# Where the operands of the matmuls lie in SBUF modulo 256 bytes, and the order of the high and low products, in a decoder layer

## The chip, the cores and the metric

The kernel runs on one core of a Trainium2 chip. The metric is the device time of one execution in microseconds, lower is better. A core has TensorE (PE: matmuls, and PEld: the loading of weights for them), VectorE (DVE), ScalarE (ACT), GpSimd (POOL) and SyncE (SP, which issues most of the DMAs here). They work from the on-chip memory SBUF, and TensorE writes its sums to PSUM.

## The reference

One step of a decoder with a single layer, for 256 prompt tokens and 8 x 4 sample tokens, all float32. Together they are 288 columns.

```
h = h + 1/2 * SwiGLU(RMSNorm(h))                    # FFN 1: 2048 -> 2 x 5632 -> 2048
z = RMSNorm(h) @ w_in                               # 2048 -> 6144 (+ 8 forget gates)
  conv group : y = B * dwconv3_causal(C * h_c)      # 1024 wide
  FoX group  : softmax(q k^T/sqrt(d) + F_t - F_s) v # 8 heads of 128; sample tokens read a paged cache of 1024
h = h + [norm(conv) | norm(FoX)] @ w_out            # 2048 -> 2048
h = h + 1/2 * SwiGLU(RMSNorm(h))                    # FFN 2
h = h + sigmoid(RMSNorm(h) @ w_g) * (p @ w_p)       # 2048 -> 2048, 256 -> 2048
y = RMSNorm(h)
```

The norms' gains are folded into the operands, and the division by the root mean square is applied behind the matmul, to its result.

## The kernel before, in words

Features lie on the 128 partitions and the 288 tokens along the row, so an operand of 2048 features is 16 blocks of 128 x 288. Each product is made at nearly full float32 precision from three faster ones in the format float32r, whose mantissa is shorter: an operand a is split into a high part (rounded to float32r) and a low part (the rest), and w x is summed as w_hi x_hi + w_hi x_lo + w_lo x_hi. `pair` (line 302) is the loop for that: for 256 output features it walks over chunks of four blocks, and in a chunk over two halves b of 128 output features and the blocks j. For each it issues the three products of lines 328, 329 and 330, each of them one matmul of 288 columns with its own load of 128 x 128 weights. Everything large goes through `pair`: both FFNs (`ffn`, line 380), the input and output projections, the last gate and its projection.

Weights come from DRAM as float32 in tiles of four blocks x 256 columns (`wraw`). `split_weight` (line 282) splits two blocks at a time: ScalarE writes the high part to a tile `whi`, VectorE the low part to a tile `wlo`. Each has five buffers of 2,048 bytes in a row of SBUF, in the pool `wsp`. In `whi` and `wlo` the weights of one matmul are 512 bytes of a row.

The moving operands are split likewise, and stand in these tiles:

- x, the input of a projection: `xh` and `xl`, 16 blocks of 1,152 bytes each (`new_x`, line 208). `make_x` and `x_split` fill them block by block, the high part on ScalarE, the low part on VectorE.
- the inner rows of the FFN: `hh` and `hl`, 8 blocks each, two buffers (`start`, line 387), filled in `up` (lines 408 and 409).
- the outputs of the two token-mixing groups, `zc` and `za`, each block a tile of its own; `zch` and `zcl` of a block are allocated one behind the other, `zah` and `zal` eight tiles of 1,152 bytes apart.
- p, the per-layer input: `ph` and `plo`.

Since 1,152 is four and a half times 256, blocks of one tile begin at 0 and at 128 modulo 256 by turns. In the program before, `whi`, `wlo`, `xh`, `xl`, `hh` and `hl` all begin at 0 modulo 256.

The order of the work is that of the program: a list of steps is run once, and each engine gets its instructions in that order. SyncE loads weights eight tiles ahead, splits run five half tiles ahead. Between the matmuls of `pair`, in the token mixing, stand small matmuls for the attention (lines 750 to 905). `inv_rms` (line 181) forms the mean of squares by a matmul with a matrix of 1/2048: `meanr` in float32r for most norms, and a constant `mean` of the same value, loaded from DRAM, in the last norm (`finish`, line 1149).

Of the kernel before, what the change touches and what calls it, by code (L numbers as in the profile page):

```python
# [16 lines left out]
F32 = mybir.dt.float32  # L17
F32R = mybir.dt.float32r
# [26 lines left out]
HALVES = 5  # L45
MANUAL = False
# [15 lines left out]
def constants():  # L62
# [15 lines left out]
    put("mean", np.full((P, P), 1.0 / D))  # L78
# [15 lines left out]
def build(nc, tc, ctx, A, O):  # L94
# [8 lines left out]
    wsp = pool("wsp", HALVES)  # L103
    drp = pool("drp", space=DRAM)
# [76 lines left out]
    def inv_rms(out, parts, width, load=True, weights=const("mean")):  # L181

        b = ktbank()
        m = b[:, :NT]
        for i, x in enumerate(parts):
            pe.matmul(m, weights, x, start=i == 0, stop=i == len(parts) - 1)
        if load:
            log_tables()
        c = float(D // width)
        s.activation(ra, m, AF.Ln, bias=eps, scale=c)  # L190
        s.activation(out, ra, AF.Exp, scale=-0.5)
        v.scalar_tensor_tensor(ra, out, -0.5 * c, out, ALU.mult, ALU.mult)
        v.scalar_tensor_tensor(ra, m, EPS / c, ra, ALU.add, ALU.mult)
        v.scalar_tensor_tensor(out, ra, 1.5, out, ALU.add, ALU.mult)

    def norm_scale(out, squares, width, chunks, load=False):

        s.activation(sqh, squares, AF.Copy)
        v.tensor_tensor(sql, squares, sqh.bitcast(F32), ALU.subtract)
        defer(lambda: inv_rms(out, [sqh, sql], width, load, meanr), chunks)  # L200
# [6 lines left out]

    def new_x():
        X["hi"] = xp.tile([P, KT, NT], F32R, name="xh", tag="xh")
        X["lo"] = xp.tile([P, KT, NT], F32R, name="xl", tag="xl")  # L210
# [55 lines left out]
    def split_upto(n):  # L266
        while state["split"] < min(n, len(halves)):
# [5 lines left out]
            lo = wsp.tile([P, 2, 256], F32R, name="wlo", tag="wlo")  # L273
# [28 lines left out]
    def pair(src, c0, kts, act, evac, k_of=lambda k: k, late=0, tag="mm", rows_first=False):  # L302
# [4 lines left out]
        for ci, ks in enumerate(chunks):  # L307
            it = weight(src, ks[0], len(ks), c0)

            def fn(ci=ci, ks=ks, it=it, only=None):  # L310
# [7 lines left out]
                for b in range(2):  # L318
                    o = st["ps"][b][:, :NT]
                    for j, k in enumerate(ks):  # L320
# [7 lines left out]
                        pe.matmul(o, hi[:, j % 2, w], xh, start=f, stop=False)  # L328
                        pe.matmul(o, hi[:, j % 2, w], xl, start=False, stop=False)  # L329
# [50 lines left out]
    def ffn(wg, wu, wd, nextgain, work):  # L380
# [3 lines left out]
        for gi, grp in enumerate(groups):  # L384
            firstg = gi == 0 and nextgain == "norm_mix"

            def start():
                H["hi"] = work().tile([P, 8, NT], F32R, name="hh", tag="hh", bufs=2)
                H["lo"] = work().tile([P, 8, NT], F32R, name="hl", tag="hl", bufs=2)
# [754 lines left out]
    def finish():  # L1144
# [3 lines left out]
        for i, c in [(0, 0), (0, 1), (1, 0), (2, 0), (1, 1), (2, 1)]:  # L1148
            pin(pe.matmul(sums[c], const("mean"), parts[i][:, SIDES[c]], start=i == 0, stop=i == 2))
# [88 lines left out]
```

## Time and profile before

| | |
|---|---|
| median of 3 runs | 2324.27 us (2323.92 to 2325.14) |
| the profiled execution | 2325.22 us |
| its span | 2323.4 us |
| TensorE busy | 2309.5 us, 99% |
| weight loads busy | 2254.4 us, 97% |
| VectorE busy | 1345.2 us, 58% |
| ScalarE busy | 1053.3 us, 45% |
| GpSimd busy | 323.4 us, 14% |
| granted TensorE clock, mean | 0.998 of full speed |
| DMA | 443.44 MB, mean 191 GB/s |

An engine's busy time is the time in which at least one of its instructions runs. Matmuls overlap in the pipeline and their ends are modelled, so a matmul's duration is longer than the time from one matmul's start to the next one's, and "99% busy" does not mean that columns stream 99% of the time. How fast matmuls follow each other is read from their start times or from their count in a window. A chain of waits follows the work back from the last instruction, at each step to what released it. `xcount` is the number of instructions in a group.

### The profile page before, as it was taken

The page shows a single profiled execution, that of the slowest core. Times are in us where ns is not written, and L with a number is a line of the kernel's source. Part 1 is how long each engine was busy: PE and PEld are TensorE (multiplying, and loading weights), DVE is VectorE, ACT ScalarE, POOL GpSimd, SP SyncE. Part 2 cuts the span into 40 slices and gives each one's busy share as a digit, 9 for nine tenths or more (in the row PEclk, how much of TensorE's full clock was granted, in tenths as well). Part 3 has the DMA queues.
Part 4 walks back from the last instruction along what each step waited for, and adds up shares of the span by engine and source line. Part 5 has one row for each costly group of instructions (what it writes and reads, how often), then busy time and mean ns, then how long its engine had stood idle before and what let it go on. Part 6 is the DMA issues. An engine that isn't in the chain of part 4 may idle for free.

```text
span 2323.4 us, 44297 instructions
## 1 busy us (share of the span) xinstructions
PE 2309.5 (99%) x17387; PEld 2254.4 (97%) x17387; DVE 1345.2 (58%) x2413; ACT 1053.3 (45%) x1860; POOL 323.4 (14%) x398
## 2 busy tenths in 40 slices
PE   9999999999999999999999999999999999999997
PEld 9999999999999999888888999999999999999997
DVE  7555555555555586456566865555555555555755
ACT  6444444444444453334344554444434444444654
POOL 1020000000000023354445210000000000000110
PEclk9999999999999999999999999999999999999999
DMA  8575555555555556888988555545555555555552
GB/s 268 165 243 164 164 166 163 169 166 164 163 165 165 168 162 232 320 302 291 325 317 294 161 169 159 173 155 172 164 167 164 169 163 164 164 165 168 164 167 92
DMA packets 342865, 443.44 MB, mean 191 GB/s; under 512 B 17424, under 2 KB 306976, under 8 KB 342656
## 3 DMA queue, kind: packets, MB, share of 16 engines
q1 hardware_dynamic: 320944, 366.32, 49.4%
q0 software_dynamic: 20480, 71.67, 8.8%
q8 instruction: 136, 2.23, 0.4%
q10 hardware_dynamic: 1232, 2.62, 0.3%
q14 instruction: 73, 0.60, 0.1%
HBM read 435.48 MB, written 5.07 MB: 190 GB/s over the span
## 4 chain that ended last, share of the span: by engine, by line
PE 99%; DVE 0%; DMA 0%; ACT 0%; SPq 0%; issue 0%; DVEq 0%; ACTq 0%
PE mm L328 31%; PE mm L330 31%; PE mm L329 31%; PE va L817 1%; PE va L750 1%; PE va L328 1%; PE va L330 1%; PE va L329 1%; DMA h<-in_x_dram 0%; DVE h L1164 0%; PE kt L328 0%; PE kt L330 0%; PE kt L329 0%; PE kt L871 0%; PE kt L904 0%; PE kt L895 0%
## 5 line engine op out<-in xcount | busy, mean ns | idle before, releaser
L283 DVE TENSOR_TENSOR wlo<-wraw,whi 128x512 fp32r<-128x512 f32 (+1 forms) x1388 | 976.0, 706 | 795.3 <-ACT whi L283 745.9
L283 ACT ACTIVATE whi<-wraw 128x512 fp32r<-128x512 f32 (+1 forms) x1388 | 868.0, 629 | 929.8 <-PE mm L329 898.0
L328 PE MATMUL mm<-xh,whi 128*128 128x288 f32 x3680 | 1093.5, 297 | 0.0
L329 PE MATMUL mm<-xl,whi 128*128 128x288 f32 x3680 | 1085.6, 295 | 0.0
L330 PE MATMUL mm<-xh,wlo 128*128 128x288 f32 x3680 | 1081.9, 294 | 0.0
L328 PEld LDWEIGHTS mm<-xh,whi 128*128 128x128 f32 x3680 | 689.3, 187 | 15.6 <-issue 13.5
L330 PEld LDWEIGHTS mm<-xh,wlo 128*128 128x128 f32 x3680 | 693.0, 188 | 0.1
L329 PEld LDWEIGHTS mm<-xl,whi 128*128 128x128 f32 x3680 | 690.6, 188 | 0.1
L328 PE MATMUL mm<-hh,whi 128*128 128x288 f32 x1408 | 416.8, 296 | 0.0
L329 PE MATMUL mm<-hl,whi 128*128 128x288 f32 x1408 | 415.4, 295 | 0.0
L330 PE MATMUL mm<-hh,wlo 128*128 128x288 f32 x1408 | 414.0, 294 | 0.0
L401 POOL TENSOR_TENSOR sr<-sg,rs 128x288 f32<-128x288 f32 x88 | 72.0, 819 | 1435.3 <-ACT sg L399 1435.1
L330 PEld LDWEIGHTS mm<-hh,wlo 128*128 128x128 f32 x1408 | 265.2, 188 | 0.0
L329 PEld LDWEIGHTS mm<-hl,whi 128*128 128x128 f32 x1408 | 264.2, 188 | 0.0
L328 PEld LDWEIGHTS mm<-hh,whi 128*128 128x128 f32 x1408 | 263.6, 187 | 0.0
L421 DVE SCALAR_TENSOR_TENSOR h<-mm,h 128x288 f32<-128x288 f32 x192 | 87.3, 455 | 23.3 <-PE mm L330 22.9
L399 ACT ACTIVATE sg<-tg 128x288 f32<-128x288 f32 x88 | 39.0, 444 | 99.3 <-DVE tg L397 99.2
L408 ACT ACTIVATE hh<-hd 128x288 fp32r<-128x288 f32 x88 | 39.2, 445 | 93.3 <-DVE hd L406 93.2
L727 POOL DMA_INDIRECT KT<-in_cache_k_dram,idx x64 | 64.2, 1003 | 117.0 <-DVE idx L162 53.5
L223 POOL TENSOR_TENSOR acc<-acc,sq 128x288 f32<-128x288 f32 x52 | 44.0, 845 | 227.2 <-ACT sq L222 224.7
L250 POOL DMA_INDIRECT page<-in_cache_v_dram,idx x64 | 64.8, 1012 | 69.5 <-PE va L817 46.3
L409 DVE TENSOR_TENSOR hl<-hd,hh 128x288 fp32r<-128x288 f32 x88 | 40.2, 457 | 22.0 <-ACT hh L408 22.0
(248 smaller groups left out, 1324.4 us busy)
## 6 DMA issues: line engine op xcount, KB each, us to landing
wraw<-in_w_ffn_gate_dram SPq DMA_DIRECT2D x172, 512.0 KB, 3.5
wraw<-in_w_ffn_up_dram SPq DMA_DIRECT2D x172, 512.0 KB, 3.5
wraw<-in_w_ffn_down_dram SPq DMA_DIRECT2D x160, 512.0 KB, 3.5
wraw<-in_w_in_dram SPq DMA_DIRECT2D x96, 512.0 KB, 5.2
wraw<-in_w_out_dram SPq DMA_DIRECT2D x32, 512.0 KB, 4.3
wraw<-in_w_ple_gate_dram SPq DMA_DIRECT2D x32, 512.0 KB, 3.5
wraw<-in_w_ffn_down_dram SPq DMA_DIRECT2D x32, 256.0 KB, 2.9
wraw<-in_w_ple_proj_dram SPq DMA_DIRECT2D x8, 256.0 KB, 3.2
```

What stands on the lines that cost most here:

```text
L223: (v if k >= KT - last_on_v else g).tensor_tensor(acc, acc, sq, ALU.add)
L250: g.indirect_dma_start(out=t, out_offset=None, in_=it["src"], in_offset=bass.IndirectOffsetOnAxis(ap=it["rows"], axis=0))
L283: for i in s.activation(hi, x, AF.Copy), v.tensor_tensor(lo, x, hi.bitcast(F32), ALU.subtract):
L328: pe.matmul(o, hi[:, j % 2, w], xh, start=f, stop=False)
L329: pe.matmul(o, hi[:, j % 2, w], xl, start=False, stop=False)
L330: state["product"] = pe.matmul(o, lo[:, j % 2, w], xh, start=False, stop=l)
L399: s.activation(u, t, AF.Silu)
L401: g.tensor_tensor(r, u, rs, ALU.mult)
L408: s.activation(H["hi"][:, k, :], t, AF.Copy)
L409: v.tensor_tensor(H["lo"][:, k, :], t, H["hi"][:, k, :].bitcast(F32), ALU.subtract)
L421: v.scalar_tensor_tensor(h[:, k, :], o, 0.5, h[:, k, :], ALU.mult, ALU.add)
L727: d = g.indirect_dma_start(out=t[:, i].rearrange("p h s -> p (h s)"), out_offset=None, in_=A["cache_k"], in_offset=bass.IndirectOffsetOnAx ...
```

## The change

The high and the low part of x become one tile, `x`, in which the high and the low part of each block lie side by side (2,304 bytes, nine times 256, from one block to the next). The function `both` makes it and returns the two views. The tile has room for a few floats ahead of the first block: 4 (16 bytes) for x and 60 (240 bytes) for the FFN's inner rows, now the tile `hid`. The low weights get a pool of their own, `wlp`, behind a gap of 8 floats (32 bytes). In the program as it is then allocated, modulo 256: every `whi` begins at 0, every `wlo` at 32, the high part of every block of `x` and `hid` at 16 and its low part at 144. The tiles of `zc`, `za` and `p` are made as before; since all that is behind the gap has moved, they begin at 32 or 160, the conv group's high parts at 32 and low parts at 160.

In `pair` the two products with the high weights change places: low x comes first, then high x, then low weights with high x. Only where blocks are asked for one by one (`rows_first`, the first pair of FFN 1) high x stays first. The constant `mean` goes, and the matmuls of the last norm read `meanr`, seen as float32, which holds the same value.

```diff
+LOWS = 8
+BEFORE_X = 4
+BEFORE_H = 60
...
-    put("mean", np.full((P, P), 1.0 / D))
...
     wsp = pool("wsp", HALVES)
+    pool("low").tile([P, LOWS], F32, name="gap")
+    wlp = pool("wlp", HALVES)
...
-    def inv_rms(out, parts, width, load=True, weights=const("mean")):
+    def inv_rms(out, parts, width, load=True):
...
-            pe.matmul(m, weights, x, start=i == 0, stop=i == len(parts) - 1)
+            pe.matmul(m, meanr, x, start=i == 0, stop=i == len(parts) - 1)
...
+    def both(p, name, blocks, before, **k):
+        n = blocks * 2 * NT
+        t = p.tile([P, (before + n + 63) // 64 * 64], F32R, name=name, tag=name, **k)
+        t = t[:, before:before + n].rearrange("p (k s n) -> p s k n", s=2, n=NT)
+        return t[:, 0], t[:, 1]
+
     def new_x():
-        X["hi"] = xp.tile([P, KT, NT], F32R, name="xh", tag="xh")
-        X["lo"] = xp.tile([P, KT, NT], F32R, name="xl", tag="xl")
+        X["hi"], X["lo"] = both(xp, "x", KT, BEFORE_X)
...
-            lo = wsp.tile([P, 2, 256], F32R, name="wlo", tag="wlo")
+            lo = wlp.tile([P, 2, 256], F32R, name="wlo", tag="wlo")
...
-                        pe.matmul(o, hi[:, j % 2, w], xh, start=f, stop=False)
-                        pe.matmul(o, hi[:, j % 2, w], xl, start=False, stop=False)
+                        for x in (xh, xl) if rows_first else (xl, xh):
+                            pe.matmul(o, hi[:, j % 2, w], x, start=f, stop=False)
+                            f = False
                         state["product"] = pe.matmul(o, lo[:, j % 2, w], xh, start=False, stop=l)
...
             def start():
-                H["hi"] = work().tile([P, 8, NT], F32R, name="hh", tag="hh", bufs=2)
-                H["lo"] = work().tile([P, 8, NT], F32R, name="hl", tag="hl", bufs=2)
+                H["hi"], H["lo"] = both(work(), "hid", 8, BEFORE_H, bufs=2)
...
-            pin(pe.matmul(sums[c], const("mean"), parts[i][:, SIDES[c]], start=i == 0, stop=i == 2))
+            pin(pe.matmul(sums[c], meanr.bitcast(F32), parts[i][:, SIDES[c]], start=i == 0, stop=i == 2))
```

TensorE has the same 16,656 products of `pair` before and after, in another order. The first place is the start of the conv half of the output projection, behind a round of the attention's values (`page`). Before:

```order
L330 MATMUL mm<-xh,wlo 128x288
L817 MATMUL va<-page,PT_13098 32x512 x8
L328 MATMUL mm<-zch_11984,whi 128x288
L329 MATMUL mm<-zcl_11985,whi 128x288
L330 MATMUL mm<-zch_11984,wlo 128x288
```

And with the change (a tile's number moves by one, and the high and low part of x bear one name, `x`):

```order
L340 MATMUL mm<-x,wlo 128x288
L826 MATMUL va<-page,PT_13097 32x512 x8
L338 MATMUL mm<-zcl_11984,whi 128x288
L338 MATMUL mm<-zch_11983,whi 128x288
L340 MATMUL mm<-zch_11983,wlo 128x288
```

The low part's product now stands ahead of the high part's with the same weights; the third product keeps its place. The second place is the end of the program on TensorE, the last block of the projection of p and the sums of the last norm. Before:

```order
L328 MATMUL mm<-ph,whi 128x288
L329 MATMUL mm<-plo,whi 128x288
L330 MATMUL mm<-ph,wlo 128x288
L1149 MATMUL kt<-acc,consts 128x144 x2
L1149 MATMUL kt<-sq_27334,consts 128x144
```

And with the change:

```order
L338 MATMUL mm<-plo,whi 128x288
L338 MATMUL mm<-ph,whi 128x288
L340 MATMUL mm<-ph,wlo 128x288
L1158 MATMUL kt<-acc,meanr 128x144 x2
L1158 MATMUL kt<-sq_27325,meanr 128x144
```

The same three products in the new order, and the sums read `meanr` for the constant. VectorE, ScalarE and GpSimd keep all their rows and their order; on SyncE the only row that differs is the load of the constants, 498 columns instead of 626.

More of the change, by code (lines that the diff above doesn't have):

```diff
@@ L199, in norm_scale @@
         v.tensor_tensor(sql, squares, sqh.bitcast(F32), ALU.subtract)
-        defer(lambda: inv_rms(out, [sqh, sql], width, load, meanr), chunks)
+        defer(lambda: inv_rms(out, [sqh, sql], width, load), chunks)
     def split(hi, lo, x, gcol):
```

## The prediction, before the result was known

> **What bounds the kernel now.** I read the summary of engines first, then the chain of work that ended last, then who waited for whom on TensorE, and then the time from one matmul to the next in stretches.
>
> ```profile
> span 2323.4 us, 44297 instructions
> PE 2309.5 (99%) x17387; PEld 2254.4 (97%) x17387; DVE 1345.2 (58%) x2413; ACT 1053.3 (45%) x1860; POOL 323.4 (14%) x398
> PE 99%; DVE 0%; DMA 0%; ACT 0%; SPq 0%; issue 0%; DVEq 0%; ACTq 0%
> ```
>
> The chain is TensorE alone. What TensorE waits for is this, from the view of waits, for the whole span:
>
> ```profile
> PE mm L509 <- DVE fixed L506: 1.2, 1, 1.2
> PE va L328 <- ACT whi L283: 0.8, 1, 0.8
> PE kt L1149 <- ACT sq L1135: 0.7, 1, 0.7
> ```
>
> That is 2.7 us in 2323.4. No wait can give or cost much, so the time is the number of matmuls times the time from one to the next, which I call the pitch. The number comes from the group of weight splits, since each split serves 2 blocks of rows and 2 output halves, 4 times three products:
>
> ```profile
> L283 ACT ACTIVATE whi<-wraw 128x512 fp32r<-128x512 f32 (+1 forms) x1388 | 868.0, 629 | 929.8 <-PE mm L329 898.0
> ```
>
> 1,388 x 4 x 3 = 16,656 matmuls of 288 columns. Their mean duration of 294 to 297 ns is a modelled pipeline time and not the pitch; the pitch is read from a window's length and the matmuls in it (the first number in brackets is TensorE's; two of each count began before the window):
>
> ```profile
> core 0: us, PE busy (x) PEld busy (x) DVE busy (x) ACT busy (x) POOL busy (x), PEclk, DMA share, GB/s
> 100.00:800.00 700.00, 700.00 (x5253) 700.00 (x5252) 377.75 (x623) 305.33 (x512) 39.82 (x46) 1.00 0.55 172
> 1312.00:1356.00 44.00, 44.00 (x332) 44.00 (x332) 38.12 (x70) 26.57 (x56) 9.43 (x12) 1.00 0.52 160
> ```
>
> 700 / 5,251 and 44 / 330 are both 133.3 ns, at a full granted clock (1.00). 16,656 x 133.3 ns = 2,220 us, 96% of the span. The question is what in 133.3 ns is neither columns nor weight load. The last norm of the kernel has matmuls of another kind, two passes over 144 columns, so again 288 column steps, with a weight load of the same 128x128 form before each pass:
>
> ```profile
> 2309.65 0.65 PE L1149 MATMUL kt<-acc,consts 128*128 128x144 f32 x4
> L1149 PE MATMUL kt<-acc,consts x4: 284/286/286, 2309.6 to 2310.0; 128*128 128x144 f32 x4
> ```
>
> Three steps fit in 0.65 us less the last one's 0.286: 121 ns. So neither 288 steps nor the weight load needs 133.3 ns; 12 ns of each of the 16,656 are something else. [...]
>
> **Does the trace before show that addresses matter?** In one stretch it does. In x and the FFN's inner rows the high and the low part stand a multiple of 256 bytes apart, so both have the same place modulo 256 (0 for even blocks, 128 for odd ones). Weights stand at 0. The conv half of the output projection is the exception: zch and zcl are 1,152-byte tiles, one behind the other, so the high part is always at 0 and the low part always at 128. Matmuls in order of time there (start, duration in us):
>
> ```profile
> 1286.69 0.29 PE L329 MATMUL mm<-zcl,whi 128*128 128x288 f32 x1
> ...
> 1288.14 0.29 PE L328 MATMUL mm<-zch,whi 128*128 128x288 f32 x1
> ...
> 1288.53 0.29 PE L328 MATMUL mm<-zch,whi 128*128 128x288 f32 x1
> ...
> 1288.93 0.30 PE L328 MATMUL mm<-zch,whi 128*128 128x288 f32 x1
> ...
> 1292.90 0.29 PE L186 MATMUL kt<-sqh,meanr 128*128 128x288 f32 x1
> ```
>
> From 1286.69 to 1292.90 there are 47 steps: 132.1 ns. Within it a block's three products take 0.39 us (1288.14 to 1288.53) where 3 x 133.3 is 0.40: 130 ns each. The attention half that follows (zah, zal: equal places again) is the 44 us window above, at 133.3 with the same engines beside it. So 133.3 is no fixed cost, and parts 128 apart run a little faster when undisturbed. When disturbed by other matmuls they can run slower. Two steps behind the attention's products (L904, L905) the view shows:
>
> ```profile
> 1251.50 0.29 PE L328 MATMUL mm<-zch,whi 128*128 128x288 f32 x1
> ...
> 1251.91 0.30 PE L328 MATMUL mm<-zch,whi 128*128 128x288 f32 x1
> 1252.04 0.31 PE L329 MATMUL mm<-zcl,whi 128*128 128x288 f32 x1
> 1252.19 0.30 PE L330 MATMUL mm<-zch,wlo 128*128 128x288 f32 x1
> 1252.33 0.29 PE L328 MATMUL mm<-zch,whi 128*128 128x288 f32 x1
> ...
> 1252.72 0.30 PE L328 MATMUL mm<-zch,whi 128*128 128x288 f32 x1
> ```
>
> The block from 1251.91 takes 0.42 us, 140 ns each, and the 9 steps from 1251.50 to 1252.72 take 135.6.
>
> [...]
>
> **The change part by part.**
>
> *Placement of x and the inner rows, of low weights, and low x first.* These act together on 16,656 pitches. The new places modulo 256: high weights 0, low weights 32, high x and inner rows 16, low ones 144 for every block. While a product streams, the next weights load. Before, the distance from loading weights to moving data was 0 or 128 in every such pair. Now it is 144 (low x, high weights coming), then -16 (high x, low weights coming), then +16 (high x, the next high weights). The trace of before shows none of these three distances. Bounds from the nearest rows: at best the excess goes, 121 ns; at worst the slow block is held, 140 ns. Rows in between: 132.1 for a whole stretch with parts 128 apart, 130 for its best blocks. The zc stretch is the nearest row, since it too has the parts 128 apart for every block; but there one distance (0) is left as it was, and here all three are moved, so I let some of the step from 132.1 to 130 be reached: 131.5 ns. 16,656 x (133.3 - 131.5) = 30 us less. Ends: 16,656 x 12.3 = 205 us less, and 16,656 x 6.7 = 112 us more.
>
> *Low x first, as a wait.* A block's first product now waits for the low part, which VectorE makes after ScalarE made the high part. The rows:
>
> ```profile
> L408 ACT ACTIVATE hh<-hd 128x288 fp32r<-128x288 f32 x88 | 39.2, 445 | 93.3 <-DVE hd L406 93.2
> L409 DVE TENSOR_TENSOR hl<-hd,hh 128x288 fp32r<-128x288 f32 x88 | 40.2, 457 | 22.0 <-ACT hh L408 22.0
> ```
>
> Before, the low part was wanted one pitch, 133 ns, after the high one. TensorE has no wait on either in the list above. The cover is the order of blocks: the last inner row is wanted in the second group of four blocks of the down projection, 24 products or 3.2 us after the first, against 0.45 + 0.46 us plus VectorE's step before. Taken at 0; with the cover gone it is 133 ns at each of the 12 groups of the two FFNs and the 3 new x, 2 us. In the kernel's first pair the old order is kept.
>
> *One tile instead of two.* High and low now share a tile, so a new x or a new set of inner rows waits for readers of both. The last reader was already the third product, which reads the high part; VectorE, ScalarE, GpSimd and SyncE keep their rows. 0.
>
> *The constant for the mean.* The table of constants loses 128 of 626 columns, and that DMA stands on SyncE behind the first weights and x. The three sums at the end read another tile with the same value. 0: no wait of TensorE in the list above is on that table, and a smaller transfer only lands earlier.
>
> *A new bound?* A split of weights serves 12 products, 1.6 us now and 1.45 at the best end of 121 ns; ScalarE needs 0.63 of it, and VectorE is 58% busy in all. DMA is at 0.52 to 0.55 in the windows. No.
>
> The sum: the profiled execution took 2325.2 us (span 2323.4 and 1.8 around it); 2325.2 - 30 = 2295, and about 2294 against the median of 2324.3. I predict 2295.
>
> **The rivals.**
>
> *The excess is a fixed cost of such a matmul.* For it: even and odd blocks stand 128 apart before, and both run at 133.3. Against it: 130 and 140 in the zc stretch. Time: 2324, no change; the same follows if the new distances happen to meet as often as the old ones. [...]
>
> *The late cycle takes hold (the other side).* Place: the streams of x and inner rows. If low at 144 and high at 16 settle into what zc shows behind an interruption, the 135.6 ns of those 9 steps hold: 16,656 x 2.3 = 38 us more, 2362. It decides from the point where slow blocks of 140 outnumber gains: 1.8 / (1.8 + 6.7), about one block in five. Against it: interruptions are rare in the FFNs, which have most matmuls, and zc comes back within 12 steps.
>
> [...]
>
> **How the numbers follow.** Forecast (a pitch of 129 to 132.6): 0.60. Fixed cost or no difference: 0.17. Late cycle: 0.14. Clash gone: 0.09. What the measurement can tell from no change is about 0.2%, 5 us. Faster by more: 0.60 + 0.09, and 0.01 from small gains outside, 0.70; same 0.16; slower 0.14. The forecast alone spans 2254 (129 ns) to 2313 (132.6 ns). The range for 8 in 10 leaves out the larger part of the late cycle and most of the vanished clash: 2225 (127.3 ns) to 2333, which takes in no change and a beginning of the late cycle.
>
> **What would show it.** Right: counts of matmuls in the same windows of 700 and 44 us go up by about 1.4%; waits of TensorE stay near 3 us; all other rows keep their durations. The fixed cost: again 5,251 in 700 us. The late cycle: blocks of 0.42 us outside the conv half. The low-first wait: a row of TensorE waiting for L409's successor. The forecast is wrong if the pitch lies outside 129 to 132.6 in the FFN stretches, or if time moves anywhere but in the pitch.

## The result, and the profile after

The changed kernel takes 2297.34 us (median of 4 runs, 2297.28 to 2297.66) against 2324.22 us for the kernel before in the same session: a ratio of 0.9884, 95% interval 0.9867 to 0.9901. 2295 us was forecast, with a range from 2225 to 2333. The profiled execution took 2297.66 us, 27.6 us less than the one of before.

The page of the changed kernel, its span, engines, chain of work and the group of weight splits (compare with the same rows in the prediction):

```profile
span 2295.9 us, 44307 instructions
...
PE 2282.3 (99%) x17387; PEld 2226.8 (97%) x17387; DVE 1346.2 (59%) x2413; ACT 1052.6 (46%) x1860; POOL 323.2 (14%) x398
...
PE 99%; DVE 0%; DMA 0%; ACT 0%; SPq 0%; issue 0%; DVEq 0%
...
L292 ACT ACTIVATE whi<-wraw 128x512 fp32r<-128x512 f32 (+1 forms) x1388 | 867.3, 629 | 907.8 <-PE mm L338 847.0
```

TensorE has the same 17,387 matmuls and the chain is still TensorE alone; the other engines work as long as before, a split still takes 629 ns. TensorE's waits in the changed kernel, for the whole span:

```profile
PE mm L518 <- DVE fixed L515: 1.2, 1, 1.2
PE kt L1158 <- ACT sq L1144: 0.7, 1, 0.7
PE kt L338 <- ACT whi L292: 0.4, 1, 0.4
```

2.3 us where it was 2.7. So the 27 us are not in waits but in the time from one matmul to the next, the pitch. Matmuls in two windows of 700 us of the changed kernel, one in FFN 1 and one in FFN 2 (the number behind "PE busy" is TensorE's count; two of each began before the window):

```profile
core 0: us, PE busy (x) PEld busy (x) DVE busy (x) ACT busy (x) POOL busy (x), PEclk, DMA share, GB/s
100.00:800.00 700.00, 700.00 (x5387) 700.00 (x5386) 392.21 (x649) 314.86 (x535) 43.02 (x50) 1.00 0.56 177
1400.00:2100.00 700.00, 700.00 (x5252) 700.00 (x5251) 380.08 (x629) 306.27 (x512) 29.22 (x36) 1.00 0.54 166
```

And the second window of the kernel before, whose first window is in the prediction (5253):

```profile
1400.00:2100.00 700.00, 700.00 (x5252) 700.00 (x5251) 380.08 (x629) 305.52 (x512) 29.29 (x36) 1.00 0.53 165
```

This is the surprise. Before, both windows run at 700 / 5,251 = 133.3 ns. After, FFN 1 runs at 700 / 5,385 = **130.0 ns** and FFN 2 at 700 / 5,250 = **133.3 ns**, the same as before the change. The code, the places modulo 256 and the order of products are the same in both FFNs. One FFN has gained 3.3 ns a matmul, the other nothing; the mean looks like the forecast. The start times of the norms' matmuls tell the same: that at the end of FFN 1 starts at 859.72 us before and at 838.39 after, 21.3 us earlier; that at the start of FFN 2 at 1357.14 and 1331.79, 25.35 earlier; and that behind FFN 2 at 2202.19 and 2176.86, 25.33 earlier.

Where the pitch changes, the timeline of TensorE in the changed kernel shows (start and duration; each L340 is the last product of a block):

```profile
1331.27 0.29 PE L340 MATMUL va<-x,wlo 128*128 128x288 f32 x1
...
1331.66 0.29 PE L340 MATMUL va<-x,wlo 128*128 128x288 f32 x1
1331.79 0.29 PE L190 MATMUL kt<-sqh,meanr 128*128 128x288 f32 x1
1331.92 0.30 PE L190 MATMUL kt<-sql,meanr 128*128 128x288 f32 x1
...
1332.33 0.30 PE L340 MATMUL va<-x,wlo 128*128 128x288 f32 x1
...
1332.73 0.30 PE L340 MATMUL va<-x,wlo 128*128 128x288 f32 x1
```

Up to the norm at 1331.79 us a block's three products take 0.39 us (1331.27 to 1331.66). Behind the norm's two matmuls they take 0.40 (1332.33 to 1332.73), and they go on so for 835 us, to the end of FFN 2, with no wait between. Each of these two ways of running repeats and holds itself; I call it a cycle. Something small at 1331.79 us chose.

FFN 1 was no different at its start. There, too, the stream ran at 130.0 when the norm's two matmuls came (x3 is three products in a row, whose duration is that of all):

```profile
38.52 0.29 PE L340 MATMUL mm<-x,wlo 128*128 128x288 f32 x1
...
38.91 0.29 PE L340 MATMUL mm<-x,wlo 128*128 128x288 f32 x1
39.03 0.29 PE L190 MATMUL kt<-sqh,meanr 128*128 128x288 f32 x1
39.17 0.30 PE L190 MATMUL kt<-sql,meanr 128*128 128x288 f32 x1
...
45.57 0.30 PE L340 MATMUL mm<-x,wlo 128*128 128x288 f32 x1
...
45.97 0.30 PE L340 MATMUL mm<-x,wlo 128*128 128x288 f32 x1
46.10 0.73 PE L338 MATMUL mm<-x,whi 128*128 128x288 f32 x3
46.67 0.30 PE L340 MATMUL mm<-x,wlo 128*128 128x288 f32 x1
...
49.29 0.29 PE L340 MATMUL mm<-x,wlo 128*128 128x288 f32 x1
...
49.68 0.29 PE L340 MATMUL mm<-x,wlo 128*128 128x288 f32 x1
```

A block takes 0.39 us before this norm and 0.40 behind it, as in FFN 2. But from 46.10 to 46.67 us three steps take 0.57 us where 0.40 is usual (the trace names no wait there), and a few blocks later the stream is back at 0.39 and stays there to the end of FFN 1. So FFN 1 has its 130.0 ns behind an irregular break 7 us after its norm, and FFN 2 met no such break. The norm's two matmuls do not always do the same: at 838.39 us they leave the stream at 130.0, and at 2176.86, behind FFN 2, they put it from 133.3 back to 130.0.

### The profile page after: what moved, and what is told of

Same layout as the page of the kernel before. It is cut to its first block, busy times and chain, and to the rows that moved or that the text cites. A ratio compares the mean times of both kernels' runs of the same rounds, so it can differ in the third digit from the quotient of the medians.

```text
span 2295.9 us, 44307 instructions
## 1 busy us (share of the span) xinstructions
PE 2282.3 (99%) x17387; PEld 2226.8 (97%) x17387; DVE 1346.2 (59%) x2413; ACT 1052.6 (46%) x1860; POOL 323.2 (14%) x398
## 4 chain that ended last, share of the span: by engine, by line
PE 99%; DVE 0%; DMA 0%; ACT 0%; SPq 0%; issue 0%; DVEq 0%
PE mm L338 62%; PE mm L340 31%; PE va L338 1%; PE va L826 1%; PE va L759 1%; PE va L340 1%; PE kt L338 0%; DMA wraw<-in_w_ffn_up_dram 0%; DVE h L1173 0%; PE kt L340 0%; PE kt L880 0%; PE kt L913 0%; PE kt L904 0%; PE kt L879 0%; PE mm L560 0%; PE va L839 0%
## 5 line engine op out<-in xcount | busy, mean ns | idle before, releaser
L338 PE MATMUL mm<-x,whi 128*128 128x288 f32 x7360 | 1459.0, 294 | 0.0
L338 PEld LDWEIGHTS mm<-x,whi 128*128 128x128 f32 x7360 | 1178.4, 188 | 15.8 <-issue 13.5
L340 PE MATMUL mm<-x,wlo 128*128 128x288 f32 x3680 | 1083.0, 294 | 0.0
L340 PEld LDWEIGHTS mm<-x,wlo 128*128 128x128 f32 x3680 | 693.0, 188 | 0.2 <-DVE wlo L292 0.2
L338 PE MATMUL mm<-hid,whi 128*128 128x288 f32 x2816 | 556.5, 294 | 0.0
L338 PEld LDWEIGHTS mm<-hid,whi 128*128 128x128 f32 x2816 | 451.4, 188 | 0.0
L340 PE MATMUL mm<-hid,wlo 128*128 128x288 f32 x1408 | 414.7, 295 | 0.0
L340 PEld LDWEIGHTS mm<-hid,wlo 128*128 128x128 f32 x1408 | 265.2, 188 | 0.0
L418 DVE TENSOR_TENSOR hid<-hd,hid 128x288 fp32r<-128x288 f32 x88 | 40.2, 457 | 22.0 <-ACT hid L417 22.0
L338 PE MATMUL va<-x,whi 128*128 128x288 f32 x256 | 51.5, 294 | 0.0
```

The costliest lines, as they stand in the source:

```text
L338: pe.matmul(o, hi[:, j % 2, w], x, start=f, stop=False)
L340: state["product"] = pe.matmul(o, lo[:, j % 2, w], xh, start=False, stop=l)
L418: v.tensor_tensor(H["lo"][:, k, :], t, H["hi"][:, k, :].bitcast(F32), ALU.subtract)
```

## The experiments

In those kernels that hold matmuls alone (the distances, the map, the sizes and the places) the decoder's work is left out and the outputs are zeros.

### The order alone

```diff
-                        pe.matmul(o, hi[:, j % 2, w], xh, start=f, stop=False)
-                        pe.matmul(o, hi[:, j % 2, w], xl, start=False, stop=False)
+                        for x in (xh, xl) if rows_first else (xl, xh):
+                            pe.matmul(o, hi[:, j % 2, w], x, start=f, stop=False)
+                            f = False
```

(This and nothing else, on the kernel before.)

> The kernel before with low x first and nothing moved. Distance theory: all distances stay 0 or 128, pitch 133.3, 2324 us. Order theory (what gains is that high x follows low x): 2297 us.

2325.62 us against 2325.83, ratio 0.9999 (0.9989 to 1.0009). Low x first costs no wait and gives nothing by itself at the old places.

### The places alone

```diff
-                        for x in (xh, xl) if rows_first else (xl, xh):
+                        for x in (xh, xl):
```

(On the changed kernel: high x first again.)

> The change with high x first. Distance theory: the distances become 16, 112, 16 instead of 144, -16, 16, so another pitch than the change's mix of 130.0 and 133.3; if 16 and 112 act as 0 does, 2324 us, if they are as good, 2297 us. Order theory: no gain without the order, 2324 us.

2304.01 us, ratio 0.9902 (0.9886 to 0.9919). No run took this median: two took 2307.10 and 2307.28 us, two 2300.69 and 2300.92. The trace is of the run of 2307.10. Its window in FFN 2 (FFN 1 has one matmul more):

```profile
1400.00:2100.00 700.00, 700.00 (x5296) 700.00 (x5295) 382.25 (x632) 307.20 (x516) 30.57 (x38) 1.00 0.53 167
```

132.2 ns in both. The places carry most of the gain, 19 to 25 us, and the order matters once the places are moved: with low x first one FFN is faster than this (130.0), the other slower (133.3). So one and the same program had two times here. What the two quicker runs did no trace shows; 6.4 us is about what one FFN, some 6,300 matmuls, would gain at 131.2 ns instead of 132.2, an estimate from the pitch that the next experiment finds for these places.

### Matmuls alone at every distance

```diff
+    def uniform(name, d):
...
+        for k in range(120):
+            mm(o, wt(0, k), mv(d, k))
...
+            for k in range(40):
+                a, b = (lo, hi) if low_first else (hi, lo)
+                mm(o, wt(0, k), mv(a, k))
+                mm(o, wt(0, k), mv(b, k))
+                mm(o, wt(wlo, k), mv(hi, k))
```

(`wt(a, k)` are weights at a modulo 256, `mv(a, k)` 288 columns of moving data at a. First all 120 at one distance, then in threes as in `pair`.)

> The kernel's work is left out here: only runs of matmuls of 288 columns with 128x128 weights in float32r, 120 to a stretch, with the moving operand at a chosen place modulo 256 behind the loading weights. Distance theory (the pitch is set by the place of the moving data against the weights that load meanwhile): the stretch with all at 0 and the one with 128 run at 133.3 ns, the change's places (low 144, high 16, low weights 32, low first) run in one of two cycles, 130.0 or 133.3, and other distances differ; two matmuls of a norm in the middle can switch the cycle, and a norm whose operands stand at the change's places, with three products, cannot. Fixed-cost theory: every stretch at 133.3. Two-pass matmuls of 144 columns: 121 ns in both.

Rows of its timeline, one for 120 matmuls in a row. dd is a distance of 48, dh 112; then threes at the change's places, threes with x at 0 and 128 and low weights at 32, and the two-pass form:

```profile
64.94 15.85 PE L131 MATMUL dd<-op 128*128 128x288 f32 x120
...
133.25 16.40 PE L131 MATMUL dh<-op 128*128 128x288 f32 x120
...
387.73 15.85 PE L131 MATMUL changex<-op 128*128 128x288 f32 x120
...
535.28 16.25 PE L131 MATMUL xzerox<-op 128*128 128x288 f32 x120
...
831.41 14.87 PE L131 MATMUL twopass<-op 128*128 128x144 f32 x120
```

A row holds a slow first step of about 0.22 us (0.13 in the last) and the last matmul's own 0.29; the start times in between give 130.0, 134.5, 130.0, 133.3 and 122.5 ns. With no other engine at work, the place of the moving data against the weights moves the pitch by 4.5 ns. The 16 distances give only a few values: 130.0, 131.1, 131.4, 131.7, 132.0, 133.3 and 134.5. A distance of 128 runs at 133.3 as expected, but a distance of 0, and threes with all at 0, run at 131.7, so the 133.3 expected there was wrong; the kernel before, whose blocks stand at 0 and 128 by turns, comes back in the last experiment. At the change's places threes run at 130.0, which FFN 1 has, also behind a pair like the norm's; nothing at these places gives the 133.3 of FFN 2 here. With high x first they run at 131.1 here, while the kernel of the experiment above holds 132.2 in its trace: already a sign that the matmuls alone and the kernel need not end in one cycle.

### Low weights back at 0

```diff
-BEFORE_H = 60
+BEFORE_H = 4
...
-    pool("low").tile([P, LOWS], F32, name="gap")
```

(Without the gap everything behind it moves back by 32 bytes, so the inner rows need 16 bytes ahead of them to stay at 16.)

> The change without the 32 bytes ahead of the low weights (x and inner rows stay at 16 and 144). Distance theory: distances 144, 16, 16; if the step of -16 carries the fast cycle, 2324 us; if only the offset of x against the weights does, 2297 us or less.

2292.18 us, ratio 0.9856 (0.9839 to 0.9872): faster than the change. Its two windows:

```profile
100.00:800.00 700.00, 700.00 (x5341) 700.00 (x5340) 386.35 (x640) 311.75 (x527) 40.79 (x47) 1.00 0.56 176
1400.00:2100.00 700.00, 700.00 (x5342) 700.00 (x5341) 384.77 (x638) 309.18 (x519) 29.04 (x36) 1.00 0.54 169
```

131.1 ns in both FFNs (alone, two of three stretches ran at 131.1 and one at 133.3). Its cycle is slower than the change's better one, but the stream keeps it, and so the whole is 5 us faster. The gap of 32 bytes, one of the three placements of the change, brings 130.0 and with it the risk.

### Nothing offset, and x alone at 0

```diff
-BEFORE_X = 4
-BEFORE_H = 60
+BEFORE_X = 0
+BEFORE_H = 0
...
-    pool("low").tile([P, LOWS], F32, name="gap")
```

> The change without the 16 bytes and the 32 bytes: high parts at 0 and low parts at 128, all weights at 0, low x first. Distance theory: as in the stretch of matmuls alone with these places, 132.2 ns, 2306 us. If the offsets carry all of the gain: 2325 us.

```diff
-BEFORE_X = 4
-BEFORE_H = 60
+BEFORE_X = 0
+BEFORE_H = 56
```

> The change without the 16 bytes ahead of x and the inner rows (0 and 128), low weights still at 32. Distance theory: as in the stretch of matmuls alone with these places, 133.3 ns, 2325 us, worse than with nothing offset. If any step away from equal places helps: 2297 to 2306 us.

With nothing offset, that is with high and low parts 128 apart in every block and low x first, 2308.09 us, ratio 0.9929 (0.9912 to 0.9946). With x at 0 and the low weights still at 32, 2324.22 us, ratio 0.9999 (0.9990 to 1.0009). Both agree with the matmuls alone (132.2 and 133.3 ns). So 16,656 x (133.3 - pitch alone) gives both within 2 us; for the places alone (131.1) it would have given 2289 against 2301 to 2307, and for the change (130.0) 2269 against 2297, since there the kernel is for a part in another cycle than the matmuls alone. Laying the parts side by side, with low x first, gives 16 us by itself. The offset of x alone gives about as much again (2292, the experiment above), the low weights' offset alone takes the 16 us away, and both offsets together bring the 130.0 that the kernel holds in one FFN.

### The norm in step: three products at chosen places

```diff
-    meanr = cst.tile([P, P], F32R, name="meanr")
+    norm = cst.tile([P, 928], F32R, name="norm")
+    meanr, meanl, sql, sqh = norm[:, 56:184], norm[:, 192:320], norm[:, 348:636], norm[:, 636:924]
...
-        for i, x in enumerate(parts):
-            pe.matmul(m, meanr, x, start=i == 0, stop=i == len(parts) - 1)
+        hi, lo = parts
+        pe.matmul(m, meanr, lo, start=True, stop=False)
+        pe.matmul(m, meanr, hi, start=False, stop=False)
+        pe.matmul(m, meanl, hi, start=False, stop=True)
```

(meanl is zero: 1/2048 has no low part. To make room, the buffer ra moves into an unused half of acc's tile. The norm's operands now lie at 0, 32, 144 and 16 modulo 256, like those of a block.)

> The change, with the norm's matmuls made like three products of a block: squares' low part at 144 and high part at 16, the mean matrix at 0, and a third product with a low matrix of zeros at 32 (its value changes nothing). Two-cycle theory (the change's stream holds 130.0 or 133.3 ns, and the two matmuls of a norm switch it): FFN 2, 837 us at 133.3 in the change, stays at 130.0, 21 us less than the change: 2276 us. If the switch has another cause (the data, a place of the weight buffers): 2297 us plus under 1 for the six products.

2276.35 us, ratio 0.9793 (0.9776 to 0.9809). Its window in FFN 2:

```profile
1400.00:2100.00 700.00, 700.00 (x5387) 700.00 (x5386) 388.55 (x645) 311.59 (x525) 30.62 (x38) 1.00 0.54 170
```

FFN 2 keeps 130.0. With one matmul more in each norm, the kernel is 21 us faster than without. It was the norm that moved the stream; whether by the places of its operands or by their number stays open here.

### Two products at the chosen places

```diff
         hi, lo = parts
         pe.matmul(m, meanr, lo, start=True, stop=False)
-        pe.matmul(m, meanr, hi, start=False, stop=False)
-        pe.matmul(m, meanl, hi, start=False, stop=True)
+        pe.matmul(m, meanr, hi, start=False, stop=True)
```

(On the version of the experiment before.)

> The changed kernel with the norm's two matmuls kept as two, but their operands moved to the places that the streams have modulo 256 (mean matrix at 0, low squares at 144, high squares at 16) and the low squares first; the third product of the run before is left out again. If it is the places of the norm's operands that put the stream from 130.0 ns to 133.3, two are enough: FFN 2 keeps 130.0 and the time is that of the version with three, 2276 (2271 to 2283). If it is the break in the row of three products that does it (two where three fit), FFN 2 goes back to 133.3 and the time is the change's, 2297 (2292 to 2303). In the matmuls alone two at these places left 130.0, so I give the first 0.65.

I gave the places 0.65, and that was wrong. 2298.11 us, ratio 0.9879 (0.9862 to 0.9895), the change's own time. FFN 2:

```profile
1400.00:2100.00 700.00, 700.00 (x5252) 700.00 (x5251) 379.46 (x629) 305.50 (x512) 29.04 (x36) 1.00 0.53 166
```

133.3 again: the chosen places with two products do not help.

### One idle matmul more, nothing moved

```diff
         m = b[:, :NT]
+        pe.matmul(b[:, NT:512], meanr, parts[0][:, :512 - NT], start=True, stop=True)
         for i, x in enumerate(parts):
             pe.matmul(m, meanr, x, start=i == 0, stop=i == len(parts) - 1)
```

(On the changed kernel. Nobody reads the 224 columns.)

> The changed kernel with one matmul more in each norm: ahead of the norm's two stands a third, 224 columns wide, into columns of the same bank of sums that nobody reads. All operands stay where they are. The last run showed the count at work: at the change's places a single matmul, of whatever width, put the stream on 133.3 ns in every second trial, and neighbouring trials differ by one in the number of matmuls run so far. If the number alone decides (three matmuls keep the step of three and the turn of odd and even, two break them), FFN 2 keeps 130.0 as in the version with three norm products at chosen places: 2276 (2271 to 2283). If that version needed its operands' places as well, FFN 2 falls to 133.3: 2297 (2292 to 2303). I give the number alone 0.7. Under the theory that only a lasting conflict of places sets the pitch there is no difference to the change either: 2297.

2277.39 us, ratio 0.9797 (0.9781 to 0.9813), 20 us under the change. The timeline at the same norm, and the window in FFN 2:

```profile
1332.30 0.29 PE L341 MATMUL va<-x,wlo 128*128 128x288 f32 x1
1332.43 0.27 PE L189 MATMUL kt<-sqh,meanr 128*128 128x224 f32 x1
1332.53 0.30 PE L191 MATMUL kt<-sqh,meanr 128*128 128x288 f32 x1
1332.68 0.29 PE L191 MATMUL kt<-sql,meanr 128*128 128x288 f32 x1
```

```profile
1400.00:2100.00 700.00, 700.00 (x5387) 700.00 (x5386) 388.64 (x646) 311.96 (x526) 30.90 (x38) 1.00 0.53 171
```

The four versions make a table:

| products in the norm | operands where they were | operands at chosen places |
|---|---|---|
| two | 2297.3 (the change) | 2298.1 |
| three | 2277.4 | 2276.4 |

For the norm ahead of FFN 2 the number decides and the places do not. A matmul that computes nothing costs 0.1 us (1332.43 to 1332.53) and keeps FFN 2 at 130.0. This is no rule that two always bring 133.3: with two at the chosen places the norm in FFN 1 leaves the stream at 130.0, and the norms around the FFNs of the changed kernel do three different things, as told with the result. With three, the stream keeps 130.0 behind the norms at the start and the end of both FFNs, in both versions. The sum fits: 835 us at 133.3 ns are some 6,260 matmuls, and 3.3 ns of each are 21 us.

### A map of places

```diff
+    for i in range(64):
+        fine("d" + L[i // 4] + "wxyz"[i % 4], 4 * i)
+    for low_first in (True, False):
+        for i in range(16):
+            for j in range(8):
+                place(("low" if low_first else "high") + L[i] + L[2 * j], 16 * i, 32 * j, low_first)
```

(`fine` runs 48 matmuls at one distance, in steps of four bytes; `place` 24 threes with high x at 16 i, low x 128 bytes from it, and low weights at 32 j.)

> The kernel's work is left out: runs of matmuls alone, 48 at each distance in steps of 4 bytes, then 72 for each place of the high part in steps of 16, of the low weights in steps of 32, in both orders, low part 128 behind the high part. Distance theory: the pitch is a fixed function of the places, between 122.5 (the two-pass rows) and 135 ns, the change's places among the best. Fixed line theory (only 16-byte lines count): steps of 4 bytes inside a line change nothing.

Over the 256 arrangements of threes the pitch is 132.5 ns in the mean, 130.0 at best and 135.6 at worst. Two of its rows (72 matmuls each; low x first, high x at 16, low weights at 32 and at 224):

```profile
605.23 9.64 PE L131 MATMUL lowbc<-op 128*128 128x288 f32 x72
...
670.24 10.01 PE L131 MATMUL lowbo<-op 128*128 128x288 f32 x72
```

The first is the change, 130.0 ns once it is in step, one of three arrangements in 256 that reach it; the second is the worst with low x first, 135.5 (the worst of all, 135.6, has high x first). All three want low x first; the best with high x first is 131.0. Steps of four bytes matter too: 4 bytes behind a multiple of 16 all distances run at 133.3 to 136.7, 12 bytes behind it 9 of 16 run at 130.0. Nothing in the map is below 130.0.

### Narrower weights, longer rows

```diff
+    def sized(name, d, n, w):
...
+        for k in range(60):
+            c = (512 * (k % 4)) // 4
+            tc.keep_in_program_order(pe.matmul(o[:w, :n], op[:, c:c + w], mv(d, k, n), start=True, stop=True))
...
+    for w in (128, 64, 32):
+        for n in (288, 384, 512):
+            for d in (0, 16, 32, 48, 112, 160):
```

(w columns of weights, n moving columns, 60 matmuls at each distance d.)

> The kernel's work is left out; only matmuls run, 60 in a row per stretch, with 128, 64 or 32 columns of weights (128, 64, 32 of them loaded per row) and 288, 384 or 512 moving columns, at six distances from moving data to loading weights modulo 256 (0, 16, 32, 48, 112, 160). If the excess over 122 ns at 288 columns is a clash of the moving read with the reading of weights, it belongs to the bytes of weights: with 64 columns of weights it is about half (4 to 6 ns instead of 8 to 11), with 32 a quarter (2 to 3), it depends on the distance while there is one, and it does not grow with the number of moving columns: 384 columns at 160 + 8 to 11 = 168 to 171 ns, 512 at 213 + 8 to 11 = 221 to 224. If the excess is a fixed cost of a matmul, it is the same for 128, 64 and 32 columns of weights and does not depend on the distance. If it is a rate of the moving read (float32r moving slower than 2.4 columns per ns), it grows with the columns: 130 x 384/288 = 173 ns and 130 x 512/288 = 231, and does not depend on the weights.

At a distance of 48, full, half and quarter weights with 288 moving columns, 60 matmuls to a row:

```profile
41.32 8.05 PE L172 MATMUL wfullad<-op 128*128 128x288 f32 x60
...
258.98 7.95 PE L172 MATMUL whalfad<-op 128*64 128x288 f32 x60
...
475.37 8.01 PE L172 MATMUL wquarterad<-op 128*32 128x288 f32 x60
```

Means over the six distances, in ns from one start to the next:

| weight columns | 288 columns | 384 | 512 |
|---|---|---|---|
| 128 | 132.4 | 174.3 | 231.8 |
| 64 | 130.2 | 173.7 | 229.5 |
| 32 | 130.9 | 172.5 | 231.1 |

A quarter of the weights takes 1.5 ns off at 288 columns where the clash would have taken some 8 off, and 0.7 at 512. (Single distances scatter by several ns: with half the weights one reaches 128.3.) And the excess grows with the columns: over the 122.5, 162.5 and 216 ns that bfloat16 takes in the next experiment it is 9.9, 11.8 and 15.8 ns with full weights. So the read of the weights is not the bulk of the 12 ns; of the three theories it is the rate of the moving read that fits, but not alone, since the distance moves the pitch. (The rate of 2.4 columns per ns, from which the expectation's 160 and 213 ns come, was not shown before; bfloat16 has it in the next experiment.)

### Which of the two places counts, fewer bytes, and the turn of odd and even

```diff
+    for d in (48, 112):
+        for s in range(0, 256, 32):
+            placed(f"shift{L[d // 16]}{L[s // 16]}", s, s + d)
+    for x_at in (48, 112):
+        for s in range(32, 256, 32):
+            placed(f"weights{L[x_at // 16]}{L[s // 16]}", s, x_at)
...
+    for i, kick in enumerate((64, 96, 128, 160, 192, 208, 224, 240, 256, 272, "two")):
+        kicked("change" + L[i], at(16), at(144), 32, True, kick)
```

(`placed` runs 60 matmuls with the weights' place and the moving data's place as its second and third argument; `kicked` runs 48 products in threes, then one matmul of `kick` columns or the norm's two, then 60 products more. The same again at the places before.)

> The kernel's work is left out; matmuls alone, 60 in a row per stretch. Since the excess did not shrink with narrower weights, the read of the weights may not be in it. Three questions. (1) Weights and moving data are both shifted by 0, 32 to 224 bytes at a constant distance of 48 and of 112, and the weights alone are shifted with the moving data at 48 and at 112. If the distance decides (the clash of my prediction), the rows with a constant distance keep 130.0 and 134.5 at all eight shifts, and shifting the weights alone changes the pitch. If the place of the moving data decides by itself, it is the other way round: the first rows change with the shift, those with the weights alone shifted keep 130.0 and 134.5. (2) bfloat16 has half the bytes per column. If the excess is in bytes of the moving read, 288, 384 and 512 columns take 121 to 123, 161 to 164 and 214 to 217 ns; if it is a fixed share of the columns, 130, 173 and 230 as in float32r. (3) 48 products at the change's places and at those before, then one matmul of another width (64 to 272 columns) or the norm's two, then 60 products at the same places. If places alone set the pitch, all eleven end on one pitch (130.0 for the change; 131.7 or 133.3 for before). If a stream has several cycles that hold themselves and the entry chooses, some end on 130.0 and some on 133.3; I expect at least two of the eleven on another cycle than the rest.

Rows of 60 matmuls. Moving data at 48 and weights at 160 or 192, so distances of 144 and 112 (weightsdk, weightsdm); moving data at 112 and weights at 64, a distance of 48 (weightshe). Then the change's places with one matmul of 64, 96 and 128 columns ahead (changeay, by, cy) and with the norm's two (changeky); the places before with one of 64; and bfloat16 with 288 and 384 columns:

```profile
198.91 8.05 PE L131 MATMUL weightsdk<-op 128*128 128x288 f32 x60
...
208.06 8.31 PE L131 MATMUL weightsdm<-op 128*128 128x288 f32 x60
...
235.88 8.06 PE L131 MATMUL weightshe<-op 128*128 128x288 f32 x60
...
325.79 8.27 PE L131 MATMUL changeay<-op 128*128 128x288 f32 x60
...
341.73 8.07 PE L131 MATMUL changeby<-op 128*128 128x288 f32 x60
...
357.44 8.27 PE L131 MATMUL changecy<-op 128*128 128x288 f32 x60
...
484.25 8.06 PE L131 MATMUL changeky<-op 128*128 128x288 f32 x60
...
500.09 8.26 PE L131 MATMUL beforeay<-op 128*128 128x288 f32 x60
...
670.05 7.51 PE L131 MATMUL short<-opb 128*128 128x288 bf16 x60
678.74 9.91 PE L131 MATMUL short<-opb 128*128 128x384 bf16 x60
```

(1) **The distance decides in most rows.** With the weights alone moved, 13 of 14 pitches are within 0.2 ns of what the list of distances has for the new distance (above, 130.0 at 144, 134.7 at 112 and 130.0 at 48); one (another distance of 144) took 131.1 for 130.0. With both moved and the distance kept, 12 of 16 keep their pitch; the others run at 132.3 to 132.7 for 130.0 (three, one of them the first row of the program) and 133.3 for 134.7 (one).

(2) **Fewer bytes.** bfloat16 takes 122.5, 162.5 and 216 ns for 288, 384 and 512 columns (of the 60 of the last row the trace holds 58): 0.417 ns a column, or 2.4 columns per ns, and 2.5 ns beside, at all three lengths. float32r with full weights has 0.444 ns a column by the table above. With half the bytes of moving data, in 288 columns of bfloat16 or in 144 of the two-pass form, a matmul takes 122.5 ns. This fits an excess in the bytes of the moving read; that it is the bytes and not the format of the operands, no run separates, and both forms ran at one set of places each.

(3) **Odd and even.** At the change's places the 60 products behind a single matmul run at 133.3 after 64, 128, 192, 224 and 256 columns and at 130.0 after 96, 160, 208, 240 and 272: every second trial, in the order in which they ran. The eleventh trial, with the norm's two, ran at 130.0 too. The number of matmuls so far differs by an odd number, 121, from each trial to the next. The pitch ahead of the single matmul was 130.0 each time. The places before, blocks at 0 and 128 by turns, give 133.3 in all 22 stretches behind and ahead, as in the kernel: one cycle only, which none of these breaks changes. (Columns were not varied apart from the order, so that they play no part is read from the alternation alone.)

## Why the prediction was right, and where it was not

**The bound: right.** TensorE alone is the chain, its waits went from 2.7 to 2.3 us, and all but that 0.4 us came from the time between matmuls.

**The excess of 12 ns as a clash of two reads, of the moving data and of the weights that load meanwhile: half right.** (Over 120 steps the two-pass form takes 122.5 ns, not the 121 read from three steps, so the excess is 11. That 144 columns of this form stand for 288 column steps is read from times: at L560 of the kernel before one float32 product of 288 columns, with 8 columns of weights, makes two passes, which take 0.65 us together and 0.41 for the second, so one starts 0.24 us behind the other, twice the 0.121; and 288 columns of bfloat16 take the same 122.5 ns as 144 of the two-pass form.) The trace of before did not show that the two reads disturb each other; the clash was the author's supposition. That the pitch depends on the distance from moving to loading data modulo 256 is shown: 13 of 14 stretches with the weights alone moved, at 130.0 ns for a distance of 144 and 134.7 for 112. But the weights' share is small. A quarter of the weights leaves most of the excess (130.9 ns for 132.4), and with half the bytes on the moving side, in bfloat16, it is gone: 122.5 ns, as in the two-pass form. An excess in the moving read fits the runs; putting the weights beside it as the cause of all 12 ns does not. In the runs with full weights and 288 columns placement moved the pitch between 130.0 and 136.7 ns, and the rest of the excess stayed.

**The term of 131.5 ns a matmul: right in the mean, wrong as a mechanism.** 27.6 us over 16,656 matmuls are 1.65 ns each, 1.8 were forecast. The step that failed is the choice of a value between 132.1 (the stretch with parts 128 apart) and 130 (its best blocks). The pitch doesn't move smoothly between: the changed kernel runs at 130.0 in one FFN and 133.3 in the other, and at 131.5 nowhere for long. By the prediction's own test (a pitch of 129 to 132.6 in the FFN stretches) FFN 1 passes and FFN 2, at 133.3, fails. The 0.39 us in the zc rows, read as best blocks that a better placement could hold, were no such thing: from 1288.14 us on the blocks take 0.39, 0.39, 0.40 and 0.40 us in turn, one cycle of 132.2 ns, the pitch that the version with nothing offset holds in both FFNs. The 130.0 of the change comes from other distances and is a cycle of its own. With FFN 2 at 130.0 as well, as one idle matmul more in each norm brings it, the time is 2277. Had FFN 1 stayed at 133.3 behind its norm, as FFN 2 did, some 6 us of the 27 would be left, since FFN 1 gave 21.3; no run shows this case. That the mean came out near the forecast is luck.

**Counts up by 1.4% in both windows: wrong in both.** The FFN 1 window went up by 2.55%. The 44 us window stands in the attention half of the output projection, whose tiles the change doesn't offset against each other; there the same length of time in the changed kernel holds fewer than the 332 of before:

```profile
1278.00:1322.00 44.00, 44.00 (x330) 44.00 (x329) 37.01 (x67) 26.25 (x55) 9.84 (x12) 1.00 0.50 160
```

44 / 328 is 134.1 ns (134.4 by the start times); everything behind the gap has moved, these tiles too. It was the wrong place for a test of this change.

**The terms taken at nothing: right.** Low x first, as a wait: 0.9999 (0.9989 to 1.0009) alone, and no row of a wait on low parts. One tile, the smaller constants (249.0 KB for 313.0) and the other reader of them: no row of theirs among the waits. That the smaller table lands earlier, as the prediction has it, no row shows.

**The rivals.** The fixed cost falls with every run that moved the pitch by place; yet x at 0 shows how near it could come, a new arrangement with 2324.2 us. The late cycle as it was named did not come: nowhere in the changed kernel do four blocks in a row, with nothing between them, run at 138 ns or more, and 133.3 rather than 135.6 is what held in FFN 2. But its form, a stream that settles into something slower behind an interruption and stays there, is what happened. The clash gone altogether, with a chance of 0.09, did not come: no long stretch of float32r with full weights and 288 columns ran under 130.0.

**What stays open.** Why a break chooses the cycle as it does: the norm's two matmuls gave 133.3 at two places of the changed kernel, left 130.0 at one and brought it back at another, and left 130.0 whenever the matmuls ran alone at these places. What the break at 46.10 us is, and what made two of four runs of the places alone quicker. Whether it is the count or its turn against the blocks' places modulo 512 that matters (blocks are nine times 256 apart). And why four-byte steps matter.

## What to carry to other kernels

Where TensorE's chain is 99% and its waits are 3 us, take the time from one matmul to the next in long windows of each stage, and compare stages that run the same code: here two values, 130.0 and 133.3 ns, meant two cycles of one stream, and what broke the stream, not the steady code, was worth tuning. Matmuls alone at the planned places tell which pitches there are, and gave two arrangements within 2 us; which of them the kernel holds they tell only with the breaks that the kernel has. Prefer a cycle that the kernel holds through its breaks (131.1 ns with the low weights at 0) to one that is faster and can be lost, or keep the breaks in step: one idle matmul of 0.1 us in each norm was worth 20.

## What the runs showed of the hardware

- Streams of float32r matmuls, 288 columns against 128 x 128 weights, fell into cycles that repeated and held for hundreds of microseconds (130.0 for 790 us, 133.3 for 835). At distances in steps of 16 the pitches were a short list (130.0, 131.1, 131.4, 131.7, 132.0, 133.3, 134.5 ns); with the weights alone moved, 13 of 14 followed the distance from moving to loading data modulo 256.
- At the change's places two cycles held, 130.0 and 133.3, and a break of a few matmuls switched the stream either way. Ahead of FFN 2 two matmuls gave 133.3 and three 130.0, at both sets of places of their operands; at other places of the kernel two left 130.0 or brought it back.
- float32r took 0.444 ns a moving column with full weights, bfloat16 0.417, at the full granted clock, and the time hardly depended on how many columns of weights were loaded (132.4, 130.2 and 130.9 ns for 128, 64 and 32).
- The best of these versions, the changed kernel with three products in the norm, takes 2276.35 us, 0.9793 (0.9776 to 0.9809) of the kernel before; with an idle third product it is 2277.39.
